# Half-precision filter weights and spectrum matrices, both orders' last filter weights prepared together, and the conditioning matmuls inside the first filter spectrum

## The chip, the core and the metric

The kernel runs on one core of a Trainium2 chip. The metric is the device time of one execution in microseconds (us). It is written with an explicit instruction stream per engine: TensorE (PE) for matmuls, with weight loads of its own (PEld), VectorE (DVE), ScalarE (ACT), GpSimd (POOL), and SyncE (SP), which here only issues DMAs. Each engine takes its instructions strictly in order, and an instruction that waits for a semaphore holds up everything behind it on the same engine.

## What is computed

A two-layer diffusion backbone over 1024 latent tokens and 256 context tokens of 1024 channels. The part that the change touches is the head of layer 0: the long filters of the Hyena half, their spectra, the conditioning vectors and the first norm.

```python
def hyena_filters(L, w1, b1, freq, w2, b2, w3):
    ...
    h = jnp.sin(freq * (z @ w1 + b1))
    h = jnp.sin(freq * (h @ w2 + b2))
    h = (h @ w3).reshape(L, 2, HY_ORDER, HY_CH)
    ...
    h = h * jnp.exp(-t01 * deltas)[:, None, None, :]
    h = h / jnp.sum(jnp.abs(h), axis=(0, 1), keepdims=True)
    ...

def long_conv(u, filt, skip):
    L = u.shape[1]
    uf = jnp.fft.rfft(u, n=2 * L, axis=1)
    ff = jnp.fft.rfft(filt, n=2 * L, axis=0)
    y = jnp.fft.irfft(uf * ff[None], n=2 * L, axis=1)[:, :L]
    return y + u * skip

def reference(x, c, ctx, c_ctx, ada_w, ada_b, norm1_g, ...):
    ...
        sh1, sc1, g1, sh2, sc2, g2 = ada_mod(c, ada_w[i], ada_b[i])
        u_lat = modulate(rms_norm(h_lat, norm1_g[i]), sh1, sc1)
    ...
            y_lat = mixer_ab(u_lat, *ab)
```

`ada_mod` is silu(c) times a 1024 x 6144 matrix. `mixer_ab` starts with an input projection of the normed and modulated tokens; two long convolutions follow (orders 0 and 1), each with a filter that does not depend on the tokens. There is one filter for the latent length ("l", 1024) and one for the context length ("c", 256), with the same weights.

## The kernel before

The filters' spectra are matmuls with stored cosine and sine matrices. To keep nearly fp32 accuracy a value is split in two parts, hi and lo (ACT copies the rounded hi, DVE subtracts it: the helper `split`, lines 287 and 289), and products are made for hi and lo apart. In this kernel the filter part works in fp32r, a rounded fp32 type of four bytes; the input projection works with pairs of f16 values.

The first 200 us of the kernel run as follows.

1. `filter_mlp`: two layers of matmul and Sin (line 592) over 640 positions, latent and context together. The result is split into `ta` and `tb` (lines 599 to 602).
2. `ada_first`: the first 2048 columns of the conditioning matrix for both conditions, 16 tiles of 512 KB from `in_ada_k`, loaded on POOL's queue into a pool of two large buffers (`mat`) and multiplied two rows at a time (line 423, 64 matmuls with 2 stationary columns). Four of its eight steps stand ahead of the raw filter, the rest are dealt into it. Then the four result rows are copied by ACT (`g`, line 431), turned into columns by 32 small matmuls, and joined with bias and gain (lines 438, 441); `operand_scale` takes the greatest entries over all partitions with an all-reduce on POOL (line 1238) and makes the scale columns that every norm needs.
3. `filter_raw` of order 0: loads the last filter weights `w3`, makes sum and difference (line 626), splits them, and for each of 4 blocks and 2 halves multiplies with `ta` or `tb` and with the window `in_win_l` (DVE, line 646).
4. `filter_spectrum` of order 0, with `filter_raw` of order 1 dealt into it, one step a yield: 16 operands (4 kinds i by 4 blocks b), each a sum or difference of two raw pieces (line 713 and its neighbours), split in hi and lo, against a 128 x 1024 matrix `in_ff_l`. That matrix comes from memory as f16 and is cast to fp32r by ACT first (line 335, into `mat`). Each order also needs a sum of absolute values over the filter, `filter_sum`: Abs on ACT (lines 658, 659), a maximum and a running sum on DVE (lines 660, 662; three sums an order), and small matmuls with a column of ones that bring it to one number per channel; DVE then inverts it (lines 678 to 681). From its twelfth step on the first norm is dealt in (`norms`: squares of the rows of x on ACT, line 2149; scaled tokens on DVE and ACT, lines 555 to 558).
5. `filter_spectrum` of order 1 with the rest of the norm.
6. `in_proj`, the input projection (f16, line 283 with `wh` and `wl`), with the context filters and more conditioning dealt into it. The context filters load `w3` again and make sum and difference on POOL (line 626) and the splits again.

All matmuls go through the helper `mm` (line 283), all SP loads through `ld` and all POOL loads through `ldr` (line 274). Names in the trace are pools: `s` holds tiles of 128x512 and 128x1024, `t` and `tk` short-lived tiles, `mat`, `wh`, `wl` large weight buffers, `c` small columns, `ps` and `pq` PSUM.

Of the kernel before, what the change touches and what calls it, by code (L numbers as in the profile page):

```python
# [19 lines left out]
P = 128  # L20
# [12 lines left out]
PAD_C, PAD_T, SHIFT = 176, 160, 16  # L33
# [168 lines left out]
class Builder:  # L202
# [117 lines left out]

    def cmat(self, w, src, view=None, small=False, shift=False):
# [86 lines left out]
    def ada_first(self):  # L408
# [7 lines left out]
        for kb in range(KB):  # L416
            ws = [self.mat(1024, F32) for _ in range(2)]
# [148 lines left out]
    def filter_mlp(self):  # L566
# [12 lines left out]
        for layer, w in enumerate((w1, w2)):  # L579
            s = self.S4(F32, 640)  # L580
            for c0, cw in ((0, 512), (512, 128)):
                ps = self.PS()
                self.mm(ps[:, :cw], w, x[:, c0:c0 + cw], True, True)
                nc.vector.tensor_scalar(s[:, c0:c0 + cw], ps[:, :cw], vec[:, layer:layer + 1], vec[:, 2:3],
                                        op0=ADD, op1=MUL)
            n = self.S4(F32, 640)
# [6 lines left out]
            x = s  # L593
        self.tap("mlp", x)
        self.ta, self.tb = {}, {}
        for sq, c0, cw in (("l", 0, 512), ("c", 512, 128)):
            ta, tb = self.S2(F32R, cw), self.S2(F32R, cw)
            cs = slice(c0, c0 + cw)
            nc.scalar.copy(ta[0:64], x[0:64, cs])
            nc.vector.tensor_tensor(ta[64:128], x[0:64, cs], ta[0:64].bitcast(F32), SUB)  # L600
            nc.scalar.copy(tb[64:128], x[64:128, cs])
            nc.vector.tensor_tensor(tb[0:64], x[64:128, cs], tb[64:128].bitcast(F32), SUB)
# [3 lines left out]
        self.alt = self.C(4, F32R)  # L606
# [3 lines left out]
        self.frg, self.rn, self.kap = {}, {}, {}  # L610

    def filter_raw(self, sq, raws, os=(0, 1)):
# [3 lines left out]
        w3, st = {}, {}  # L616
        for o in os:
            for j in (0, 1):
                st[(o, j)] = self.S2()
                self.ld(st[(o, j)], a["w3"][:, (2 * j + o) * HC:(2 * j + o + 1) * HC])  # L620
        if sq == "l":
            yield
        for o in os:
            for eo, op in ((0, ADD), (1, SUB)):
                t = self.T()
                (nc.vector if sq == "l" else nc.gpsimd).tensor_tensor(t, st[(o, 0)], st[(o, 1)], op)
                hi, lo = self.S2(F32R), self.S2(F32R)
                self.split(t, hi, lo)
                w3[(o, eo)] = (hi, lo)
        for b in range(nb):  # L630
            for s, lh in ((0, self.ta[sq]), (1, self.tb[sq])):
                w = self.S2()
                self.ld(w, a["win_" + sq][b, s])
# [16 lines left out]
    def filter_sum(self, sq, o, raw):  # L650
# [3 lines left out]
        if sq == "l":  # L654
            acc = self.S4()
            for b in range(nb):
# [4 lines left out]
                if b:  # L661
                    nc.vector.tensor_tensor(acc, acc, t, ADD)
# [21 lines left out]
    def filter_spectrum(self, sq, o, raw):  # L684
# [8 lines left out]
        fh = (self.S2(F32R), self.S2(F32R))  # L693
        nc.scalar.copy(fh[0][0:1, :], re[0:1, :])
        nc.vector.tensor_tensor(fh[1][0:1, :], re[0:1, :], fh[0][0:1, :].bitcast(F32), SUB)
# [5 lines left out]
        def operands():  # L701
            for i in range(4):
                for b in range(nb):
# [8 lines left out]
                    else:  # L712
                        (nc.vector if sq == "l" else nc.gpsimd).tensor_tensor(t, f, r, ADD if i in (0, 3) else SUB)
# [1408 lines left out]
    def run(self):  # L2122
# [17 lines left out]
        def norms():  # L2140
# [6 lines left out]
            with self.follow(self.last_hi):  # L2147
                for i, t in rows:
                    nc.scalar.activation(t, t, AF.Square, accum_out=sq[:, i:i + 1])
# [42 lines left out]
        mlp, fr = self.filter_mlp(), self.filter_raw("l", raws["l"], (0,))  # L2192
# [3 lines left out]
        next(fr)  # L2196
        next(ng)
        drain(mlp)
        for _ in range(4):
            next(ada1)  # L2200
        with self.tc.issue_after(self.clamp), self.tc.issue_after(self.sin):
            next(fr)
        for i, _ in enumerate(fr):
            next(ada1, None)
            if i in (0, 4):
                next(ng)
        drain(ada1)
        self.u0col, self.usi = self.operand_scale(0, 0, (0, 1))
# [303 lines left out]
```

## Time and profile before

| what | us |
|---|---|
| median of the runs shown (2914.33, 2919.48, 2921.39) | 2919.48 |
| the profiled execution | 2919.95 |
| its span | 2918.2 |
| PE busy over the span | 2766.6 (95%) |
| DVE busy | 2094.0 (72%) |
| ACT busy | 1647.7 (56%) |
| POOL busy | 642.6 (22%) |
| first spectrum's first matmul | 69.44 |
| second spectrum's first matmul | 140.74 |
| input projection's first matmul | 205.69 |

Times in the trace count from the span's start. Rows of a timeline give start, duration, engine, line of the kernel, operation, output and inputs by pool names, shapes and count, and in brackets how long the engine stood idle just before and what released it. Rows of stretches give the busy time of each engine with its number of instructions, then the clock that TensorE was granted as a share of full speed, the busy share of the DMA engines and GB/s. Matmul ends are modelled, so a row of one matmul shows its latency; the pace is read from the starts of successive rows.

### The profile page before, as it was taken

The page shows a single profiled execution, that of the slowest core. Times are in us where ns is not written, and L with a number is a line of the kernel's source. Part 1 is how long each engine was busy: PE and PEld are TensorE (multiplying, and loading weights), DVE is VectorE, ACT ScalarE, POOL GpSimd, SP SyncE. Part 2 cuts the span into 40 slices and gives each one's busy share as a digit, 9 for nine tenths or more (in the row PEclk, how much of TensorE's full clock was granted, in tenths as well). Part 3 has the DMA queues.
Part 4 walks back from the last instruction along what each step waited for, and adds up shares of the span by engine and source line. Part 5 has one row for each costly group of instructions (what it writes and reads, how often), then busy time and mean ns, then how long its engine had stood idle before and what let it go on. Part 6 is the DMA issues. An engine that isn't in the chain of part 4 may idle for free. (4 is left out here: it accounts for less than half of the span.)

```text
span 2918.2 us, 46050 instructions
## 1 busy us (share of the span) xinstructions
PE 2766.6 (95%) x16163; PEld 1714.2 (59%) x16163; DVE 2094.0 (72%) x3833; ACT 1647.7 (56%) x2899; POOL 642.6 (22%) x1057
## 2 busy tenths in 40 slices
PE   6989999999989999999999999999999999999998
PEld 3766557888879644444555844676665444444554
DVE  4778867585467798877886767776676778775765
ACT  4674324454675667654555555676664477654553
POOL 1012013354220121213120012444443022112000
PEclk8989999999999999999999999999999999999999
DMA  6574434358785555566994798777775666424753
GB/s 254 187 265 161 161 122 151 111 168 286 285 344 182 207 205 197 201 213 240 327 333 161 273 337 294 179 188 172 185 198 188 236 226 231 153 93 184 242 191 113
DMA packets 325156, 615.98 MB, mean 211 GB/s; under 512 B 90934, under 2 KB 130552, under 8 KB 324922
## 3 DMA queue, kind: packets, MB, share of 16 engines
q1 hardware_dynamic: 252378, 384.38, 39.9%
q0 software_dynamic: 70240, 224.45, 21.6%
q10 hardware_dynamic: 2304, 4.20, 0.4%
q8 instruction: 127, 2.08, 0.3%
q14 instruction: 107, 0.88, 0.1%
HBM read 455.33 MB, written 135.53 MB: 202 GB/s over the span
## 5 line engine op out<-in xcount | busy, mean ns | idle before, releaser
L1449 PE MATMUL ps<-s,s 128*128 128x512 f16 x2592 | 582.2, 382 | 14.4 <-ACT tk L1454 6.8
L1449 PEld LDWEIGHTS <-s 128*128 128x128 f16 x2640 | 259.0, 98 | 332.6 <-issue 27.8
L283 PE MATMUL ps<-s,wh 128*128 128x256 f32 (+3 forms) x1752 | 398.2, 331 | 11.1 <-ACT wh L287 5.4
L1218 ACT ACTIVATE s<-s,c 128x512 f16<-128x512 f32 (+1 forms) x324 | 233.5, 754 | 141.9 <-DMA s<-d 79.9
L1219 DVE SCALAR_TENSOR_TENSOR s<-s,c,s 128x512 f16<-128x512 f32 (+1 forms) x324 | 247.4, 794 | 84.5 <-ACT s L1218 84.1
L1666 PE MATMUL ps<-s 128*128 128x512 f16 (+2 forms) x1308 | 303.4, 378 | 2.0 <-DVE s L1219 2.0
L283 PE MATMUL pq<-s,wh 128*128 128x512 f16 (+1 forms) x1000 | 280.3, 354 | 9.8 <-DMA wh<-d 5.4
L283 PE MATMUL ps<-s,wl 128*128 128x256 f32 (+3 forms) x876 | 261.6, 331 | 1.3 <-DVE wl L289 1.2
L283 PEld LDWEIGHTS <-wh 128*128 128x128 f16 x1664 | 160.9, 99 | 170.2 <-issue 20.9
L1666 PEld LDWEIGHTS <-s 128*128 128x128 f16 x1536 | 148.5, 98 | 178.9 <-issue 6.5
L274 POOL DMA_DIRECT2D d<-s x201 | 109.0, 543 | 640.5 <-DVE s L1510 178.6
L283 PE MATMUL ps<-s,s 128*128 128x65 f16 (+5 forms) x2666 | 222.3, 236 | 27.5 <-DMA s<-s 11.4
L335 ACT CAST mat<-cs 128x1024 fp32r<-128x1024 f16 (+2 forms) x120 | 111.6, 935 | 140.6 <-PE ps L283 57.3
L283 PEld LDWEIGHTS ps<-s,wh 128*128 128x128 f32 x1088 | 177.5, 192 | 18.1 <-ACT wh L287 5.7
L283 PE MATMUL ps<-s,mat 128*128 128x512 f32 x696 | 184.7, 413 | 3.3 <-DVE s L289 2.9
L1449 PE MATMUL ps<-s,wh 128*128 128x512 f16 x616 | 184.9, 379 | 1.8 <-DVE g L1463 1.4
L283 PE MATMUL pq<-s,wl 128*128 128x512 f16 (+1 forms) x500 | 174.5, 354 | 0.5 <-DMA wl<-d 0.5
L283 PEld LDWEIGHTS <-s 128*128 128x128 f16 x2400 | 114.5, 98 | 82.9 <-DMA s<-s 11.5
L283 PEld LDWEIGHTS ps<-s,mat 128*128 128x128 f32 x696 | 136.5, 199 | 37.9 <-DVE s L289 3.8
L1251 ACT ACTIVATE t<-s 128x1024 bf16<-128x1024 f32 (+1 forms) x164 | 141.9, 867 | 12.2 <-DVE c L470 8.4
L283 PEld LDWEIGHTS ps<-s,s 128*128 128x128 f32 (+1 forms) x746 | 113.6, 192 | 32.1 <-ACT s L287 7.0
L283 PEld LDWEIGHTS <-wl 128*128 128x128 f16 x832 | 82.3, 99 | 77.4 <-issue 4.5
(431 smaller groups left out, 5477.3 us busy)
## 6 DMA issues: line engine op xcount, KB each, us to landing
s<-d SPq DMA_DIRECT2D x294, 256.0 KB, 4.0
d<-s POOLq DMA_DIRECT2D x157, 256.0 KB, 3.2
s<-in_down SPq DMA_DIRECT2D x154, 256.0 KB, 5.4
s<-in_ada_w POOLq DMA_DIRECT2D x48, 512.0 KB, 4.8
g<-in_bias POOLq DMA_DIRECT2D x128, 192.0 KB, 3.6
s<-in_gate SPq DMA_DIRECT2D x46, 512.0 KB, 3.7
s<-in_up SPq DMA_DIRECT2D x46, 512.0 KB, 4.0
d<-g POOLq DMA_DIRECT2D x87, 256.0 KB, 2.9
```

What stands on the lines that cost most here:

```text
L274: self.last_ldr = self.nc.gpsimd.dma_start(out, in_).ins
L283: self.nc.tensor.matmul(o, l, r, start=st, stop=sp)
L335: self.nc.scalar.copy(m, st)
L1218: nc.scalar.activation(hi, src, AF.Copy, scale=scale)
L1219: nc.vector.scalar_tensor_tensor(lo, src, scale, hi, op0=MUL, op1=SUB)
L1251: self.nc.scalar.activation(junk[:, :t.shape[1]], t, AF.Abs, scale=2.0 ** -15, accum_out=st[:, k:k + 1])
L1449: nc.tensor.matmul(ps, x[:, sl], y, start=first and j == 0 and x is wh and y is xh, stop=j == 3 and x is wl, skip_group_check=True)
L1666: m = nc.tensor.matmul(acc[j][:, c0:c1], x[:, sl], y[:, xs], start=first and k == 0, stop=last and k == 2, skip_group_check=True)
```

## The change

Types: `ta`, `tb`, the alternating signs and the splits of the filter part become f16 (`split16`: hi and lo halves of one f16 tile), and `in_ff_l` is loaded as f16 straight into the matmul's buffer (`mat16`, three buffers) without a cast. The casts of line 335 fall away for the filters' matrices: 32 for the latent ones, and small ones for the context.

Weights: a new `filter_w3` loads `w3` of both orders and the first two windows, finds a scale from the column sums of absolute values (Abs on ACT, matmuls with ones, a maximum on DVE), makes the four sums and differences on DVE, splits them into f16 pairs, and writes these to device memory (`w3d`) through POOL's queue. `filter_raw` takes them from there; the context filters read `w3d` back and prepare nothing.

Order: `ada_first` is dealt into the first eight steps of the first spectrum, with buffers from the large `s` pool in place of `mat`; its end and `operand_scale` follow at the ninth. The squares of the norm go one by one where the program puts them. The running sum of `filter_sum` moves from DVE to POOL, and so do the sums of order 1 in blocks 0 and 2 that have no mask (5 of 16).

```diff
-PAD_C, PAD_T, SHIFT = 176, 160, 16
+PAD_C, PAD_T, SHIFT = 168, 160, 16
...
+    def mat16(self, w):
+        self.m16 = (getattr(self, "m16", 0) + 1) % 3
+        return self.pw.tile([P, w], F16, tag=("ws", "wh", "wl")[self.m16], name=self.nm("m16"))
...
-            ws = [self.mat(1024, F32) for _ in range(2)]
+            ws = [self.S4() for _ in range(2)]
...
-        self.sgn = self.S2(F32R)
+        self.sgn = self.S2(F16)
...
+        self.w3d = {(o, eo): self.DR([P, 1024], F16) for o in (0, 1) for eo in (0, 1)}
+
+    def split16(self, src):
+
+        t = self.S2(F16, 1024)
+        self.nc.scalar.copy(t[:, :512], src)
+        self.nc.vector.tensor_tensor(t[:, 512:], src, t[:, :512], SUB)
+        return t[:, :512], t[:, 512:]
+
+    def filter_w3(self):
...
+        for o in (0, 1):
+            ab = self.T(BF16, 1024)
+            ps = sums[o] = self.PS()
+            for j in (0, 1):
+                nc.scalar.activation(ab[:, j * 512:j * 512 + 512], st[(o, j)], AF.Abs)
+            for j in (0, 1):
+                self.mm(ps, self.ones.bitcast(BF16)[:, 1::2], ab[:, j * 512:j * 512 + 512], j == 0, j == 1)
+        yield
...
+        for o in (0, 1):
             for eo, op in ((0, ADD), (1, SUB)):
                 t = self.T()
+                nc.vector.tensor_tensor(t, st[(o, 0)], st[(o, 1)], op)
+                x = self.S2(F16, 1024)
+                self.half_split(t, big[:, o:o + 1], x[:, :512], x[:, 512:])
+                self.ldr(self.w3d[(o, eo)], x)
+                self.w3[(o, eo)] = (x[:, :512], x[:, 512:])
+            yield
...
                 if b:
-                    nc.vector.tensor_tensor(acc, acc, t, ADD)
+                    nc.gpsimd.tensor_tensor(acc, acc, t, ADD)
...
-                        (nc.vector if sq == "l" else nc.gpsimd).tensor_tensor(t, f, r, ADD if i in (0, 3) else SUB)
-                    xh, xl = self.S2(F32R), self.S2(F32R)
-                    self.split(t, xh, xl)
-                    yield xh, xl, self.cmat(2 * nb * P, a["ff_" + sq][i, b])
+                        eng = nc.vector if sq == "l" and (o == 0 or b % 2) else nc.gpsimd
+                        eng.tensor_tensor(t, f, r, ADD if i in (0, 3) else SUB)
+                    xh, xl = self.split16(t)
+                    mt = self.mat16(2 * nb * P)
+                    self.ld(mt, a["ff_" + sq][i, b])
+                    yield xh, xl, mt
...
         fr = self.filter_raw("l", raws["l"], (1,))
         for i, _ in enumerate(self.filter_spectrum("l", 0, raws["l"][0])):
+            if i < 8:
+                next(ada1)
+            elif i == 8:
+                drain(ada1)
+                self.u0col, self.usi = self.operand_scale(0, 0, (0, 1))
             if i >= 2:
                 next(fr, None)
-            if i >= 11:
+            if i < 4 or i >= 11:
                 next(ng)
```

On ACT, at the head of the program, before (`s_44` and `s_48` are the states of the two filter layers, the rows of line 2149 the squares of the norm):

```order
L592 ACTIVATE s_44_142<-s_44_142 128x640
L592 ACTIVATE s_48_157<-s_48_157 128x640
L599 CAST s_52_172<-s_48_157 64x512
L601 CAST s_53_173<-s_48_157 64x512
L599 CAST s_54_178<-s_48_157 64x128
L601 CAST s_55_179<-s_48_157 64x128
L287 CAST s_71_225<-t_223 128x512
L287 CAST s_74_231<-t_229 128x512
L2149 ACTIVATE s_34_122,c_265<-s_34_122 128x1024
```

The second Sin stands right behind the first, and the squares come after the splits. Now, in the same place (Sin is line 598, the squares line 2200, the hi copy of `ta` line 607):

```order
L2200 ACTIVATE s_42_138,c_241<-s_42_138 128x1024
L598 ACTIVATE s_48_150<-s_48_150 128x640
L2200 ACTIVATE s_43_140,c_241<-s_43_140 128x1024
L2200 ACTIVATE s_44_142,c_241<-s_44_142 128x1024
L2200 ACTIVATE s_45_144,c_241<-s_45_144 128x1024
L2200 ACTIVATE s_46_146,c_241<-s_46_146 128x1024
L2200 ACTIVATE s_47_148,c_241<-s_47_148 128x1024
L2202 ACT_TABLE_LOAD
L2202 ACTIVATE c_241<-c_241,c_95 128x10
L598 ACT_TABLE_LOAD
L598 ACTIVATE s_58_182<-s_58_182 128x640
L607 CAST s_62_197<-s_58_182 64x512
```

The first Sin stands among the squares, and the second behind all ten of them, a square root and two table loads.

On POOL, behind the conditioning loads, before (line 1238 is the all-reduce, its first row sets the engine up for it):

```order
L274 DMA mat_329<-in_ada_k 128x1024
L1238 ISA
L1238 ISA c_425<-c_425 128x1
L274 DMA s_553_1698<-in_cg_l 128x256 x2
L626 ISA
L626 TENSOR_TENSOR t_1831<-s_588_1823,s_589_1825 128x512
L626 TENSOR_TENSOR t_1837<-s_588_1823,s_589_1825 128x512
L626 TENSOR_TENSOR t_1843<-s_590_1827,s_591_1829 128x512
L626 TENSOR_TENSOR t_1849<-s_590_1827,s_591_1829 128x512
```

The all-reduce is the only computation on POOL until line 626, in the input projection. Now (line 711 is the running sum of order 0 in `s_238`, line 1290 the all-reduce, line 764 sums of order 1):

```order
L274 DMA s_227_706<-in_ada_k 128x1024
L711 TENSOR_TENSOR s_238_734<-s_238_734,s_256_815 128x1024
L1290 ISA
L1290 ISA c_783<-c_783 128x1
L711 ISA
L711 TENSOR_TENSOR s_238_734<-s_238_734,s_264_850 128x1024
L711 TENSOR_TENSOR s_238_734<-s_238_734,s_269_875 128x1024
L764 TENSOR_TENSOR t_1086<-s_208_663 128x512
L764 TENSOR_TENSOR t_1223<-s_208_663 128x512
L764 TENSOR_TENSOR t_1274<-s_150_456 128x512
L764 TENSOR_TENSOR t_1350<-s_210_668 128x512
```

The all-reduce stands between the first and the second sum of order 0, and the engine is set up for it and set back in between.

On PE, toward the end of the first spectrum, before (`ps_973` is the column sum of the running sum `s_254_779`, `s_300` and `s_301` hi and lo of an operand):

```order
L283 MATMUL ps_932<-s_300_936,mat_942 128x512
L283 MATMUL ps_933<-s_300_936,mat_942 128x512
L283 MATMUL ps_973<-c_91,s_254_779 128x1 x8
L283 MATMUL pq_930<-s_301_937,mat_942 128x512
L283 MATMUL pq_930<-s_300_936,mat_942 128x512
L283 MATMUL ps_931<-s_301_937,mat_942 128x512
L283 MATMUL ps_931<-s_300_936,mat_942 128x512
L283 MATMUL ps_932<-s_301_937,mat_942 128x512
L283 MATMUL ps_932<-s_300_936,mat_942 128x512
```

The running sum comes from DVE, and 32 matmuls of the first spectrum stand behind the column sum. Now (`ps_948` is the column sum, `s_289_943` hi and lo of the operand):

```order
L283 LDWEIGHTS m_290_946
L283 MATMUL ps_913<-s_289_943,m_290_946 128x512
L283 LDWEIGHTS m_290_946
L283 MATMUL ps_914<-s_289_943,m_290_946 128x512
L283 MATMUL ps_948<-c_91,s_238_734 128x1 x8
L283 LDWEIGHTS m_290_946
L283 MATMUL ps_911<-s_289_943,m_290_946 128x512
L283 LDWEIGHTS m_290_946
L283 MATMUL ps_911<-s_289_943,m_290_946 128x512
L283 LDWEIGHTS m_290_946
L283 MATMUL ps_912<-s_289_943,m_290_946 128x512
```

The column sum, which now waits for the last of POOL's three sums, stands ahead of the last 20 matmuls of the first spectrum.

More of the change, by code (lines that the diff above doesn't have):

```diff
@@ L585, in filter_mlp @@
                                         op0=ADD, op1=MUL)
+            if layer == 0:
+                yield
             n = self.S4(F32, 640)
@@ L593, in filter_mlp @@
             x = s
+            if layer == 0:
+                yield
         self.tap("mlp", x)
@@ L2146, in norms @@
             sq = self.C(10)
-            with self.follow(self.last_hi):
-                for i, t in rows:
-                    nc.scalar.activation(t, t, AF.Square, accum_out=sq[:, i:i + 1])
+            for i, t in rows:
+                nc.scalar.activation(t, t, AF.Square, accum_out=sq[:, i:i + 1])
+                yield
             nc.scalar.activation(sq, sq, AF.Sqrt, scale=1.0 / D, bias=self.eps)
```

84 lines of the change are left out of this document (51 added, 33 removed).

## The prediction

> **What bounds the kernel now.** The change works at the head, so I read the table of stretches first, cut at the first matmul of each stage.
>
> ```profile
> core 0: us, PE busy (x) PEld busy (x) DVE busy (x) ACT busy (x) POOL busy (x), PEclk, DMA share, GB/s
> 0.00:42.50 42.50, 19.63 (x70) 8.66 (x70) 22.26 (x40) 20.18 (x40) 9.21 (x23) 0.90 0.95 360
> 42.50:69.40 26.90, 21.20 (x73) 10.88 (x72) 6.02 (x25) 9.68 (x17) 1.97 (x4) 0.65 0.37 118
> 69.40:140.70 71.30, 64.00 (x258) 50.13 (x258) 51.16 (x86) 43.88 (x64) 0.00 (x0) 0.90 0.51 169
> 140.70:198.20 57.50, 54.53 (x226) 42.22 (x227) 49.39 (x77) 46.99 (x70) 1.28 (x2) 0.94 0.65 223
> 198.20:211.60 13.40, 6.07 (x18) 2.56 (x18) 4.74 (x10) 10.13 (x18) 2.94 (x2) 0.62 1.01 382
> 211.60:460.00 248.40, 241.02 (x1340) 138.08 (x1339) 194.78 (x406) 86.55 (x155) 41.12 (x50) 0.98 0.42 152
> ```
>
> Up to 42.5 us the DMA engines are full (0.95). From 42.5 to 69.4 no engine but PE is busy, with 73 matmuls in 27 us at a granted clock of 0.65. Then two spectra of 71.3 and 57.5 us, in which DVE has 51 and 49 us of work beside PE. From 211.6 on PE is the bound (241 of 248 us), and what the head gains passes on almost unchanged. The timeline of ACT and PE tells what the second stretch is.
>
> ```profile
> 24.05 0.74 ACT L592 ACTIVATE s<-s 128x640 f32<-128x640 f32 x1 [7.56 <-DVE s L591]
> 27.42 0.79 PE L283 MATMUL ps<-s,s 128*128 128x512 f32 x1 [5.86 <-ACT s L287]
> 32.38 1.90 PE L423 MATMUL ps<-mat,c 128*2 128x512 f32 x16
> 52.37 3.08 PE L423 MATMUL ps<-mat,c 128*2 128x512 f32 x8 [2.91 <-DMA mat<-in_ada_k]
> 56.21 6.96 PE L283 MATMUL ps<-c,g 2*128 2x2 f32 x32 [0.77 <-ACT g L431]
> 63.10 1.22 PE L283 MATMUL ps<-t,c 128*128 128x256 f32 x2
> 64.11 3.62 PE L283 MATMUL ps<-tk,c 128*128 128x512 f32 x4
> 69.44 0.39 PE L283 MATMUL ps<-s,c 128*2 128x512 f32 x1 [0.51 <-ACT s L287]
> ```
>
> The raw products start 3.4 us after the second Sin; then PE waits for the conditioning tiles one after the other, up to 55.4, turns the rows into columns, and only then starts the first spectrum. So 42.5 to 69.4 is a chain of latencies, not work.
>
> **The change, part by part.**
>
> *The front.* The second Sin now stands behind ten squares of the norm, a root and two table loads. A square is 1.05 us and a load 1.28 us here:
>
> ```profile
> 27.79 1.06 ACT L2149 ACTIVATE s<-s 128x1024 f32<-128x1024 f32 x1
> L413 ACT ACT_TABLE_LOAD x1 | 1.3, 1283 | 0.7 <-PEq L2499 0.7
> GB/s 0 32 217 349 373 392 359 247 415 418 423 418 421 423 412 420 407 411 411 418 410 388 402 395 406 396 421 330 104 16 74 295 341 343 232 105 8 5 0 31
> s<-in_x_row SPq DMA_DIRECT2D x10, 512.0 KB, 9.8
> 5.57 10.73 SPq L268 DMA_DIRECT2D s<-in_x_row  x10
> ```
>
> The tenth row of x is what matters. Ahead of it on SP's queue stand now 1.0 MB more of w3 and windows, but the conditioning tiles no longer share the DMA engines: they wait on POOL's queue behind the w3d writes. About 7.5 MB (ten rows of 0.52 MB, six tiles of 0.26 MB, the rest small) have to land; the slices of 1.5 us of the first 60 us in the DMA view add up to this at about 22.8 us; square, loads and root (1.05 + 0.2 + 1.28 + 0.3 + 1.28) put the Sin at 27.0, 3 us later than now. From there the raw products start 3.4 us later as now, two more pairs are split on DVE (1.4), 16 window products follow (0.62 apart: 9.9), then the first row's pieces and the operand sums that stand ahead in DVE's queue (some 7 us of ten instructions like L713), and hi, lo and their waits (3.3): 52.0 us for the first spectrum's start instead of 69.44. The preparation of w3 (four Abs, matmuls with ones, sums and splits) lies ahead of the second Sin, where ACT waited 7.56 us and PE 5.86; it costs nothing while w3 lands before the rows of x, and each us of delay beyond that costs one. If the tenth row lands as late as now plus the added bytes (issued at 16.3 us, 9.8 us to landing, then 1.0 MB at 415 GB/s, 2.5: 28.6), the Sin comes at 32.7 and the start at 58.
>
> *To the first running sum.* Now DVE makes the first of these at 116.40, 46.96 after the spectrum's start. What comes in: 64 conditioning matmuls at 0.12 us (1.90 for 16: 7.6); the columns and the row sums, which took 6.96 and 1.22 + 3.62 at clock 0.65 and take 0.65/0.95 of it at full clock (8.1); some 2 us of waits in their chain PE, ACT, PE, DVE. What goes out: f16 in place of fp32r.
>
> ```profile
> 100.98 2.96 PE L283 MATMUL ps<-s,mat 128*128 128x512 f32 x12
> 103.78 1.56 PE L283 MATMUL pq<-s,mat 128*128 128x512 f32 x6
> 213.01 0.59 PE L283 MATMUL ps<-s,wl 128*128 128x512 f16 x2
> 213.55 0.59 PE L283 MATMUL ps<-s,wh 128*128 128x512 f16 x2
> L335 ACT CAST mat<-cs 128x1024 fp32r<-128x1024 f16 x32 | 33.4, 1051 | 34.0 <-issue 12.4 <-PE ps L283 10.4 <-PE ps L423 5.2
> ```
>
> Twelve fp32r matmuls take 2.80 us (0.233 each); three f16 ones of 1280 columns together 0.54 (0.216 per 512). So 185 matmuls save 3.1 us; the type alone is worth little, since f16 and fp32r run at nearly one pace. The 32 casts (33.4 us) leave ACT, which was never the last to be waited for by much; that is worth something only where ACT holds DVE up. First running sum: 52 + 46.96 + 7.6 + 8.1 + 2 - 3.1 = 113.6 us.
>
> *The sums and the all-reduce on POOL.* This is what the change adds. Its prices:
>
> ```profile
> 476.64 2.55 POOL L901 TENSOR_TENSOR t<-t,t 128x512 f32<-128x512 f32 x2 [22.36 <-DVE t L900]
> 413.33 1.79 POOL L848 TENSOR_TENSOR s<-s,s 128x512 f32<-128x512 f32 x1
> 420.85 0.38 POOL L1238 PARTITION_ALL_REDUCE c<-c  x1 [5.73 <-issue]
> 421.26 0.15 DVE L1239 TENSOR_SCALAR c<-c 128x1 f32<-128x1 f32 x1 [6.13 <-POOL c L1238]
> 431.07 1.27 POOL L852 TENSOR_TENSOR s<-s 128x128 f32<-128x128 f32 x1 [9.85 <-issue]
> L662 DVE TENSOR_TENSOR s<-s,s 128x1024 f32<-128x1024 f32 x6 | 7.3, 1211 | 0.0
> ```
>
> A 512-wide sum is 1.27 us on POOL, so a 1024-wide one is about 2.55 (DVE: 1.21). Where an all-reduce follows a tensor operation, POOL stands 5.73 us with nothing to wait for, and DVE waits 6.13 for it. In the head of the kernel before, this set-up is hidden, since POOL does nothing else there. Now the first sum stands ahead of it and two more behind it. DVE does only some 4 us of work meanwhile and then stops at the reduce's result, with eight pieces of the norm and the lo halves of the last two operands behind it, for which PE waits. From the first sum (0): sum to 2.55, set-up to 8.28, reduce to 8.66; DVE goes on, norms start at about 9.2 (at 122.8; now 122.14). Setting POOL back for the sums is priced nowhere: between 0.1 us (nothing) and 5.7 us (as much as the other way; the 9.85 us ahead of 431.07 hold other waits too and don't tell). I take half, 2.9. The second and third sum end at 8.66 + 2.9 + 5.1 = 16.7. PE's column sum waits for this, at the head of PE's queue, with 20 matmuls (4.3 us) behind it; with 1.0 us for the column sum the second spectrum starts at 113.6 + 22.0 = 135.6 us, with the bounds 132.8 and 138.4. That is 5.1 us before the 140.74 of now: of 17.4 us gained in front, 12.3 are given back.
>
> [...]
>
> *The second spectrum.*
>
> ```profile
> 140.74 0.39 PE L283 MATMUL ps<-s,c 128*2 128x512 f32 x1 [2.70 <-ACT s L287]
> L713 DVE TENSOR_TENSOR t<-s 128x512 f32<-128x512 f32 x24 | 16.0, 680 | 0.0
> L626 POOL TENSOR_TENSOR t<-s,s x4: 1266/1760/2246, 208.7 to 213.3; 128x512 f32<-128x512 f32 x4
> 211.15 1.09 DVE L289 TENSOR_TENSOR s<-t,s 128x512 fp32r<-128x512 f32 x1 [1.80 <-ACT s L287]
> 212.17 2.29 DVE L470 CUSTOM_DVE_ANT_0 s<-s,s 128x1024 f32<-128x1024 f32 x1
> 214.39 2.28 DVE L470 CUSTOM_DVE_ANT_0 t<-s,s 128x1024 bf16<-128x1024 f32 x1
> 218.41 1.21 DVE L470 CUSTOM_DVE_ANT_0 s<-s,s 128x1024 f32<-128x1024 f32 x1
> ```
>
> DVE works 49.4 of 57.5 us now and is the bound together with its waits for ACT. It loses three sums (1.21) and five operand sums (0.68): 7.0. But POOL's operations slow it: while POOL made four 512-wide sums, three DVE instructions took 1.09, 2.29 and 2.28 us instead of 0.68, 1.21 and 1.21, that is 2.6 us, or 0.64 a sum. Five of these and three of double width cost 7.0: a draw. The 8.1 us in which DVE was not busy should shrink, since 16 casts of 1.05 us leave ACT's 47 us and hi copies come sooner; I take 4.6. So 49.4 + 4.6 = 54 us, and the end is 135.6 + 54 = 189.6 instead of 198.2: 8.6 us.
>
> *The input projection.* Four POOL sums with their slowing of DVE (2.6) and four lo parts on DVE (2.7) go. PE's waits for DVE there are these:
>
> ```profile
> PE ps L283 <- DVE c L1316: 3.8, 1, 3.8
> PE ps L867 <- DVE s L289: 3.4, 1, 3.4
> ```
>
> Between nothing and 3.8 us of that goes; I take 2.5, as the work is spread over more than these two places. The rest of the kernel keeps its order but for small shifts: nothing, within 2 us.
>
> **Sum.** 8.6 + 2.5 = 11.1 us against the profiled execution of 2919.95 us (0.5 us over the median of the runs shown): 2908.9, so 2909 us. Its own range, from the bounds of setting back, of the projection and of the shifts: 2903 to 2916.
>
> **Rivals.**
>
> *ACT was what held DVE up.* For it: both waits of PE before the spectra end at ACT's hi copies (2.70 us at 140.74), and 33 us leave ACT. Then the second spectrum runs at DVE's bare 49.4 us, setting back is free (132.8), and it ends at 182.2: 16.0 gained, and 3.8 in the projection: 2900. Against it: the norms' chain DVE, ACT, DVE stays.
>
> *The tenth row of x comes late.* The Sin at 32.7 as above, the spectrum's start at 58: 6 us less gain, 2915. For it: DMA is full in that time; against it: the conditioning tiles, 8.4 MB, start later than now.
>
> *POOL costs more than it saves: slower.* The place is POOL from its first sum to the end of the second spectrum. Setting back takes 5.7 us (start at 138.4), and each POOL sum blocks DVE for its whole length, 5 x 1.27 + 3 x 2.55 = 14.0 instead of 7.0, while DVE's idle 8.1 us stay, as the norms wait for ACT and DMA as before: 42.4 + 14.0 + 8.1 = 64.5. The end is at 202.9, 4.7 us later than now; the projection gives nothing: 2925. It decides from a second spectrum of 60 us on. For it: POOL itself took up to 2.25 us for 1.27. Against it: DVE's 2.29 for 1.21 are less than a whole sum.
>
> [...]
>
> **How the numbers follow.** Below 0.3% (8.8 us) a measurement of this kernel can't be told from no change; the forecast lies just beyond it. Chances: forecast 0.45, ACT relief 0.17, late row 0.13, POOL dearer 0.20, and 0.05 for shifts elsewhere. Faster by over 0.3% (below 2911): 0.27 of the forecast's 0.45, 0.17 of the relief, 0.02 more: 0.46. Slower by over 0.3% (above 2929): 0.10 of POOL dearer (late row and POOL together give 2931) and 0.03 more: 0.13. The rest is 0.41. The range takes in the relief and the POOL case: 2898 to 2927.
>
> **What would show it.** Right: the first spectrum starts at 50 to 55 us; DVE stands about 4 to 5 us before the reduce's result; PE stands before the column sum for several us; the second spectrum starts at 133 to 138 and lasts about 54 us. Wrong: a second Sin after 31 us (late row); a second spectrum under 51 us (relief) or over 60 (POOL); a gap between the reduce and the second sum of under 1 us or over 6; or the input projection growing.

## The result and the profile after

The change makes the kernel slightly slower. Over 20 runs each, the median is 2923.16 us (2915.45 to 2932.81) against 2913.79 us before (2905.21 to 2925.07); the ratio is 1.0028 with a 95% interval of 1.0018 to 1.0038, about 8 us. The profiled execution took 2932.81 us (span 2931.0), the highest of the 20, so stages are compared here at places in the head, not by the span.

The stretches of the profile after, cut at the first matmul of each stage and at PE's waits between the spectra (columns as in the stretches of before):

```profile
0.00:50.90 50.90, 17.34 (x44) 6.29 (x45) 31.80 (x58) 26.82 (x48) 9.76 (x24) 0.97 0.88 322
50.90:120.00 69.10, 68.30 (x298) 25.46 (x297) 30.06 (x52) 26.56 (x44) 3.15 (x6) 0.92 0.57 193
120.00:131.70 11.70, 4.99 (x25) 2.33 (x25) 6.89 (x17) 1.13 (x3) 2.72 (x2) 0.93 0.21 67
131.70:141.60 9.90, 1.86 (x4) 0.40 (x3) 5.25 (x12) 1.72 (x4) 5.50 (x3) 0.50 0.00 0
141.60:154.00 12.40, 10.56 (x36) 6.02 (x37) 3.33 (x10) 3.08 (x7) 1.18 (x1) 0.64 0.21 71
154.00:213.90 59.90, 53.95 (x226) 22.16 (x226) 52.23 (x71) 35.67 (x57) 23.37 (x9) 0.89 0.64 213
213.90:221.80 7.90, 0.35 (x3) 0.04 (x2) 0.66 (x5) 7.90 (x16) 0.00 (x0) 0.80 1.03 417
221.80:470.00 248.20, 243.92 (x1354) 137.93 (x1355) 193.90 (x407) 83.81 (x147) 36.20 (x47) 0.97 0.46 159
```

The first spectrum starts at 50.9 us instead of 69.4. But from 120.0 to 141.6 PE runs 29 matmuls in 21.6 us, and from there to 154.0 only 36 more; the granted clock is 0.50 from 131.7 on and 0.64 in the last of these stretches. From 131.7 to 141.6 no engine is busy for more than 5.5 of the 9.9 us: it is a chain of waits, the same picture that 42.5 to 69.4 gave before, in another place. The timeline of POOL names it:

```profile
120.08 2.34 POOL L711 TENSOR_TENSOR s<-s,s 128x1024 f32<-128x1024 f32 x1 [38.19 <-issue]
128.75 0.38 POOL L1290 PARTITION_ALL_REDUCE c<-c  x1 [6.33 <-issue]
136.02 5.55 POOL L711 TENSOR_TENSOR s<-s,s 128x1024 f32<-128x1024 f32 x2 [6.89 <-issue]
```

The first running sum, 6.33 us in which POOL waits for nothing on record, the all-reduce, 6.89 us of the same, and two more sums up to 141.57. What hangs on it, on DVE and on PE:

```profile
120.78 1.73 DVE L1286 SCALAR_TENSOR_TENSOR c<-c 128x1 f32<-128x1 f32 x2
129.16 0.15 DVE L1291 TENSOR_SCALAR c<-c 128x1 f32<-128x1 f32 x1 [4.31 <-POOL c L1290]
145.23 0.16 DVE L727 COPY c<-ps 128x4 f32<-128x4 f32 x1 [8.28 <-PE ps L283]
```

```profile
50.93 0.58 PE L283 MATMUL pq<-s,c 128*2 128x512 f16 x1 [6.56 <-ACT s L624]
120.28 4.71 PE L283 MATMUL ps<-s,m 128*128 128x512 f16 x21
131.74 1.86 PE L283 MATMUL ps<-s,m 128*128 128x512 f16 x4 [6.76 <-ACT s L624]
141.62 3.57 PE L283 MATMUL ps<-c,s 128*128 128x1 f32 x16 [8.01 <-POOL s L711]
145.05 7.12 PE L283 MATMUL ps<-s,m 128*128 128x512 f16 x20
154.01 0.38 PE L283 MATMUL pq<-s,c 128*2 128x512 f16 x1 [1.84 <-ACT s L624]
221.76 2.31 PE L283 MATMUL ps<-s,wh 128*128 128x256 f16 x6 [1.72 <-ACT wh L1270]
```

DVE stops for the reduce, and with it the operands of the spectrum: PE stands 6.76 us. Then PE stands 8.01 us for the last sum on POOL, and DVE 8.28 us for PE. The 20 matmuls that the program has behind the column sum stand with it: the last hi and lo halves made for them (lines 624 and 625) were done at 132.2 and 135.2 us, and they start at 145.05. When PE goes on, its granted clock is 0.50 (141.6 to 145.05): the column sum takes 3.57 us, and 20 f16 matmuls take 7.12 us, where 20 at the pace of before take 4.3. (e1 below shows that the second of these two prices doesn't hang on the long stops.) So the 18.5 us gained in front turn into 13.3 us lost at the second spectrum's start (154.01 against 140.74) and 16.1 at the projection's start (221.76 against 205.69). The projection up to the first matmul of line 919 (line 867 before) takes 248.2 us instead of 254.0, which leaves 10.3 us. That is the measured loss within its uncertainty.

### The profile page after: what moved, and what is told of

Same layout as the page of the kernel before. It is cut to its first block, busy times and chain, and to the rows that moved or that the text cites. A ratio compares the mean times of both kernels' runs of the same rounds, so it can differ in the third digit from the quotient of the medians.

```text
span 2931.0 us, 45984 instructions
## 1 busy us (share of the span) xinstructions
PE 2765.4 (94%) x16167; PEld 1664.1 (57%) x16167; DVE 2087.2 (71%) x3822; ACT 1614.8 (55%) x2860; POOL 665.1 (23%) x1068
## 3 DMA queue, kind: packets, MB, share of 16 engines
q0 software_dynamic: 70560, 225.37, 21.7%
## 5 line engine op out<-in xcount | busy, mean ns | idle before, releaser
L1501 PEld LDWEIGHTS <-s 128*128 128x128 f16 x2640 | 258.7, 98 | 328.4 <-issue 22.5
L283 PE MATMUL ps<-s,wh 128*128 128x256 f32 (+3 forms) x1848 | 406.0, 328 | 10.8 <-ACT wh L287 7.8
L283 PE MATMUL ps<-s,wl 128*128 128x256 f32 (+3 forms) x924 | 268.5, 328 | 1.2 <-DVE wl L289 1.2
L283 PE MATMUL pq<-s,wh 128*128 128x512 f16 (+1 forms) x904 | 254.4, 362 | 5.5 <-DVE s L2007 2.4
L1718 PEld LDWEIGHTS <-s 128*128 128x128 f16 x1536 | 148.4, 98 | 179.0 <-issue 6.5
L283 PEld LDWEIGHTS <-s 128*128 128x128 f16 (+1 forms) x2500 | 124.6, 98 | 109.4 <-issue 23.6
L283 PE MATMUL pq<-s,wl 128*128 128x512 f16 (+1 forms) x452 | 159.8, 362 | 0.0
L1270 ACT ACTIVATE s<-t,c 128x512 f16<-128x512 f32 x174 | 116.3, 711 | 21.1 <-DVE c L1369 9.8
L339 ACT CAST mat<-cs 128x1024 fp32r<-128x1024 f16 (+2 forms) x80 | 74.7, 941 | 94.8 <-PE ps L283 27.5
L1271 DVE SCALAR_TENSOR_TENSOR s<-t,c,s 128x512 f16<-128x512 f32 x174 | 124.9, 747 | 1.6 <-ACT s L1270 1.6
L1501 PE MATMUL ps<-s,wl 128*128 128x512 f16 x308 | 116.5, 379 | 0.0
```

The lines of the kernel that those rows point to most:

```text
L283: self.nc.tensor.matmul(o, l, r, start=st, stop=sp)
L339: self.nc.scalar.copy(m, st)
L1270: nc.scalar.activation(hi, src, AF.Copy, scale=scale)
L1271: nc.vector.scalar_tensor_tensor(lo, src, scale, hi, op0=MUL, op1=SUB)
L1501: nc.tensor.matmul(ps, x[:, sl], y, start=first and j == 0 and x is wh and y is xh, stop=j == 3 and x is wl, skip_group_check=True)
L1718: m = nc.tensor.matmul(acc[j][:, c0:c1], x[:, sl], y[:, xs], start=first and k == 0, stop=last and k == 2, skip_group_check=True)
```

## The experiments

Eleven runs of ten kernels were made, each beside the kernel before on the same chip. The table gives the starts of the two last stages of the head and of the first matmul of line 919 or its counterpart, from one profile each, and the ratio of the times to before. "Reduce early" and the other names are explained below.

| kernel | second spectrum | projection | line 919 | ratio to before (95%) |
|---|---|---|---|---|
| before | 140.74 | 205.69 | 459.7 | |
| the change | 154.01 | 221.76 | 470.0 | 1.0028 (1.0018 to 1.0038) |
| e1, all running sums on DVE | 142.34 | 207.49 | 456.1 | 0.9971 (0.9957 to 0.9986) |
| e2, order 0's sums on DVE | 141.10 | 209.15 | 457.2 | 1.0018 (1.0004 to 1.0032) |
| e9, the same again | 141.76 | 209.89 | 459.9 | 1.0027 (1.0012 to 1.0042) |
| e12, two of order 0's sums on DVE | 148.69 | 216.55 | 463.8 | 1.0039 (1.0025 to 1.0054) |
| e4, operand sums on DVE | 151.89 | 223.99 | 473.1 | 1.0067 (1.0050 to 1.0084) |
| e5, reduce early | 134.15 | 202.60 | 452.1 | 0.9968 (0.9955 to 0.9982) |
| e6, reduce early, sums on DVE | 134.35 | 199.32 | 448.5 | 0.9954 (0.9938 to 0.9971) |
| e11, reduce early, all on DVE | 134.38 | 199.44 | 449.7 | 0.9959 (0.9944 to 0.9975) |
| e8, conditioning in front | 141.55 | 209.70 | 458.4 | 0.9997 (0.9987 to 1.0008) |
| e7, before with sums on POOL | 134.33 | 203.90 | 457.2 | 1.0031 (1.0016 to 1.0045) |
| e10, before with f16 spectra | 133.67 | 197.01 | 448.0 | 0.9995 (0.9978 to 1.0012) |

The theory: POOL's set-up for the all-reduce and back, with the running sums around it, is on the path of DVE and PE and costs what the front gained. Its main rival: POOL's sums and DVE hold each other up, spread over both spectra.

### All running sums on DVE (e1)

```diff
-                    nc.gpsimd.tensor_tensor(acc, acc, t, ADD)
+                    nc.vector.tensor_tensor(acc, acc, t, ADD)
```

> All six running sums back on DVE, all else as in the change. Theory (POOL's set-up, reduce, set-back and two sums, 21.5 us from the first sum to the column sum, hold DVE and PE): the column sum comes at about 127 us instead of 141.6, PE does not cool down, the second spectrum starts at about 136 instead of 154.0, and the time falls by 14 to 18 us against the change, to about 6 to 8 us below the kernel before. [...] Rival (what is gained in front is lost in the projection whatever happens in between): under 4 us.

The ratio goes from 1.0028 to 0.9971, 16.6 us: the theory's 14 to 18. In the profiles 11.7 us of it stand at the second spectrum's start and 13.9 at line 919. The column sum comes at 127.64 (PE's timeline):

```profile
127.64 1.91 PE L283 MATMUL ps<-c,s 128*128 128x1 f32 x16
133.35 7.16 PE L283 MATMUL ps<-s,m 128*128 128x512 f16 x20 [1.92 <-DVE s L625]
142.34 0.38 PE L283 MATMUL pq<-s,c 128*2 128x512 f16 x1 [1.84 <-ACT s L624]
```

The second spectrum starts 6 us later than expected: the 20 matmuls behind the column sum still take 7.16 us, as in the change (7.12), so that the expected "PE does not cool down" was wrong: the granted clock falls here, too. The stretches of this run show that the long stops aren't needed for it:

```profile
112.00:120.00 8.00, 7.23 (x36) 4.90 (x35) 3.96 (x11) 7.75 (x11) 0.00 (x0) 0.68 0.56 191
133.30:140.60 7.30, 7.16 (x20) 2.54 (x20) 6.04 (x13) 1.36 (x3) 1.57 (x1) 0.62 0.12 36
```

The clock is low from the conditioning's 32 small column matmuls on (0.68), and again after two stops of only 0.86 and 1.92 us (0.62). Behind the column sum it falls in before and in e11, too, where PE stood only 2.61 and 1.03 us ahead of it: 0.50 from 129 to 132 us in before, 0.79 from 120 to 128 in e11. What the long stops of the change add to this is the column sum at a granted clock of 0.50, 3.57 us instead of 1.91.

### Order 0's sums on DVE, twice (e2, e9)

```diff
-                    nc.gpsimd.tensor_tensor(acc, acc, t, ADD)
+                    (nc.gpsimd if o else nc.vector).tensor_tensor(acc, acc, t, ADD)
```

> Only order 0's three running sums back on DVE; order 1's stay on POOL. Theory: nearly all of the loss stands between the first and the second spectrum, so 12 to 16 us below the change and within 5 us of the run with all six on DVE; the second spectrum keeps its 60 us. [...]

> Order 0's sums on DVE once more, beside the others on one chip. In its profile the input projection started only 1.7 us later than with all six on DVE, while its median was 12.7 us higher. Theory (the rest is spread of TensorE's granted clock after the head): now within 6 us of all six on DVE, about 0.1 to 0.2% below the kernel before. If order 1's sums on POOL cost something real further down: again 0.1 to 0.3% above it.

A miss, twice, and on two chips. In the head the theory holds: the second spectrum starts at 141.10 and 141.76, the projection some 2 us after e1's. But the medians stay at 1.0018 and 1.0027: of e1's 16.6 us below the change no more than 3, and the second is the number of e9's rival (again 0.1 to 0.3% above before). What makes the difference comes for the greater part after the projection's start. The granted clock lies between 0.975 and 0.984 from run to run, and within the runs of e2 and of e9 a difference of 0.002 goes with 2 and 4 us. This stays open, below.

### Two of order 0's three sums on DVE (e12)

```diff
-                    nc.gpsimd.tensor_tensor(acc, acc, t, ADD)
+                    (nc.vector if o == 0 and b < 3 else nc.gpsimd).tensor_tensor(acc, acc, t, ADD)
```

> Order 0's first two running sums on DVE, the third on POOL, where it stands ahead of the all-reduce; order 1's stay on POOL. So the set-up for the reduce stays on DVE's path and the set-back goes off the column sum's path. Theory: DVE stands 6 to 8 us before the reduce's result (2.5 us sum, 5.7 to 6.3 us set-up), the column sum comes at about 129 us, the second spectrum starts at 146 to 149, between the change (154.0) and order 0's sums all on DVE (141.1 and 141.8). If only the set-back and the late column sum hurt: the second spectrum starts within 2 us of 141.5.

This takes the set-up for the reduce apart from the set-back. Rows of the timelines of POOL, DVE and PE:

```profile
125.73 2.34 POOL L711 TENSOR_TENSOR s<-s,s 128x1024 f32<-128x1024 f32 x1 [43.48 <-PE ps L283]
134.20 0.38 POOL L1290 PARTITION_ALL_REDUCE c<-c  x1 [6.13 <-issue]
134.61 0.15 DVE L1291 TENSOR_SCALAR c<-c 128x1 f32<-128x1 f32 x1 [8.95 <-POOL c L1290]
137.20 1.86 PE L283 MATMUL ps<-s,m 128*128 128x512 f16 x4 [7.13 <-ACT s L624]
148.69 0.38 PE L283 MATMUL pq<-s,c 128*2 128x512 f16 x1 [1.84 <-ACT s L624]
```

One sum ahead of the reduce, and DVE stands 8.95 us (6 to 8 were expected), PE 7.13 behind it. The second spectrum starts at 148.69, inside the expected 146 to 149: the set-up with one sum is worth 7.3 us against e2 and e9 (141.4), the set-back with the other two sums 5.3 us more. The total time doesn't follow: 1.0039 is no lower than the change's 1.0028, although line 919 comes 6.1 us earlier.

### The reduce early (e5), and with the sums on DVE too (e6)

```diff
-            if i < 8:
+            if i < 4:
                 next(ada1)
-            elif i == 8:
+                next(ada1)
+            elif i == 4:
                 drain(ada1)
```

> The conditioning steps go two to a step of the first spectrum, and the all-reduce comes at its fifth step, ahead of all running sums, which stay on POOL. Theory: set-up and set-back (6.3 and 6.9 us) are hidden, the three sums remain; the second spectrum starts at about 141 (13 us earlier), and the time falls by 10 to 13 us against the change. If POOL's slow sums and not the set-ups are the cost: 3 to 5 us only. If the conditioning tiles arrive too late for this order: PE waits for them in the first 30 us of the spectrum.

> The early all-reduce and all six running sums on DVE together. Theory: with the reduce early, set-up and set-back are hidden already, so taking the sums off POOL adds only what the column sum still waits (0.5 us) and the 3 us that order 1's sums on POOL cost the second spectrum: 2 to 5 us below the early reduce alone. If the set-ups are not the cost but the sums: as much gain as the sums on DVE brought to the change, 13 to 17 us.

With POOL still making all sums, but the reduce ahead of them, the ratio is 0.9968, 17.5 us below the change; the expected 10 to 13 was too low. POOL's and PE's rows of e5:

```profile
96.04 0.38 POOL L1290 PARTITION_ALL_REDUCE c<-c  x1 [37.37 <-DVE c L1289]
112.45 9.24 POOL L711 TENSOR_TENSOR s<-s,s 128x1024 f32<-128x1024 f32 x3 [16.03 <-PE ps L283]
134.15 0.38 PE L283 MATMUL pq<-s,c 128*2 128x512 f16 x1 [1.84 <-ACT s L624]
```

The reduce starts as soon as its input is there, at 96.0, and 16 us pass before the first sum is wanted: both set-ups are hidden. The second spectrum starts 19.9 us earlier than in the change, and not all of that is POOL's. From the first running sum to the second spectrum e5 takes 21.7 us and the change 33.9: 12.2 less, near the expected 13. Another 6.6 come ahead of the first running sum, which stands 62.5 us behind the first spectrum's start instead of 69.15, and 1.0 from the front. The earlier conditioning is part of the edit: its 64 matmuls stand in larger groups and keep PE busy for 10.9 us instead of 13.8.

With the sums on DVE as well (e6) it is 0.9954, some 4 us less, as expected: 3.3 us of it show at the projection's start, though the two intervals overlap. This is the lowest ratio of the study, 13 us below before.

The four kernels together take the two parts of the edit apart. With the reduce late, POOL's sums cost 11.7 us at the second spectrum's start (154.01 in the change, 142.34 in e1); with the reduce early, nothing (134.15 in e5, 134.35 in e6). And where POOL makes no running sum at all, the early conditioning with its reduce still brings that start from 142.34 to 134.35, 1.1 of it from the first spectrum's start.

### Operand sums on DVE (e4, e11)

```diff
-                        eng = nc.vector if sq == "l" and (o == 0 or b % 2) else nc.gpsimd
+                        eng = nc.vector if sq == "l" else nc.gpsimd
```

e4 is the change with this edit, e11 is e6 with it.

> Only the operand sums of order 1 back on DVE; the running sums stay on POOL. Theory: the set-up, the reduce and the order 0 sums stand as they are, the second spectrum starts at 154 as in the change; 0 to 3 us faster than the change. [...]

> Early all-reduce, running sums and operand sums all on DVE: POOL has nothing but the reduce until the projection. Theory: the run with only the operand sums on DVE lost 4.4 us in its second spectrum against the change, so five operand sums on POOL are a gain; 2 to 5 us slower than the early reduce with the running sums on DVE. [...]

The main rival falls in this place: without POOL's five operand sums the second spectrum up to the projection takes 72.1 us in e4 against 67.75 in the change, longer and not shorter. The theory missed, too: 0 to 3 us faster were expected, and e4's median, 1.0067, loses 11 us against the change, of which 3.1 show at line 919. In e11 the price is 1 us or so, a little under what was expected, and the second spectrum up to the projection is no longer than in e6 (65.06 and 64.97).

### Before with the sums on POOL (e7)

```diff
-                    nc.vector.tensor_tensor(acc, acc, t, ADD)
+                    nc.gpsimd.tensor_tensor(acc, acc, t, ADD)
```

> The kernel before with one part of the change alone: the six running sums on POOL. The all-reduce stands ahead of them by 50 us there. Theory: set-up and set-back stay hidden, DVE gains 3.6 us an order and loses about as much by sharing: within 4 us of before. Rival (sums on POOL cost by themselves): 8 us or more slower than before.

```profile
59.07 0.38 POOL L1238 PARTITION_ALL_REDUCE c<-c  x1 [12.05 <-DVE c L1237]
112.15 5.77 POOL L662 TENSOR_TENSOR s<-s,s 128x1024 f32<-128x1024 f32 x2 [1.23 <-DVE s L660]
117.97 2.08 PE L283 MATMUL ps<-c,s 128*128 128x1 f32 x16 [1.31 <-POOL s L662]
```

In the profile the set-ups are hidden and the column sum waits 1.31 us, no more. In that execution the conditioning came early and the first spectrum started at 63.90 instead of 69.44; from there to the projection it took 140.0 us against 136.25, 3.8 more, inside the expected 4. (The loss by "sharing" in this expectation is an estimate from the prediction's rows around 212 us of before, 0.64 us of DVE for each 512-wide sum on POOL, so 3.8 for an order's three of double width.) The median is 9 us above before, though, which is the rival's number. The profiled execution was the fastest of 12 (2913.19 us, median 2926.38), so the profile can't settle it.

### The conditioning in front again (e8)

```diff
         for i, _ in enumerate(self.filter_raw("l", raws["l"], (0,))):
+            next(ada1, None)
...
+        drain(ada1)
+        self.u0col, self.usi = self.operand_scale(0, 0, (0, 1))
```

The same steps are left out of the first spectrum.

> The change with the conditioning dealt into the raw filter of order 0 again, ahead of the first spectrum, and the all-reduce with it; sums stay on POOL. The first spectrum starts at 66 to 72 us, since the conditioning tiles are loaded behind the w3 writes. If the place of the conditioning is worth what its matmuls and columns cost inside the spectrum (15 and 6 us, against the 17 to 20 us of waiting in front): within 5 us of the early reduce. If the front gain is real and kept: 10 us or more slower than the early reduce.

The last conditioning tile is used at 62.23 and the first spectrum starts at 69.25, 19.3 us after e5's. Yet the second starts only 7.4 us after e5's, and the ratio is 0.9997 against 0.9968, 8.5 us. Neither expectation hits; the truth lies between: of the gain in front more than half is spent again on the conditioning's matmuls and columns inside the spectrum, and some 7 us are kept. Part of these 7 is another wait: PE stands 4.71 us for POOL's last sum before e8's column sum, and 0.53 in e5.

### Before with f16 in the spectra alone (e10)

```diff
-                    xh, xl = self.S2(F32R), self.S2(F32R)
-                    self.split(t, xh, xl)
-                    yield xh, xl, self.cmat(2 * nb * P, a["ff_" + sq][i, b])
+                    xh, xl = self.split16(t)
+                    mt = self.mat16(2 * nb * P)
+                    self.ld(mt, a["ff_" + sq][i, b])
+                    yield xh, xl, mt
```

with f16 signs, and with w3 and the raw products left in fp32r.

> The kernel before with the spectra's types alone: operands and matrices in f16, no casts of the matrices; conditioning, sums, w3 and order stay as before, and w3 and the raw products stay fp32r. Theory (as in the prediction): the pace of a matmul is nearly the same, 480 of them save at most 8 us of PE time, and ACT is freed of 33 us that were hidden: 3 to 8 us faster, most of it in the second spectrum. Rival (ACT held DVE up): the second spectrum runs at DVE's 49 us, and 10 us or more are gained. Rival (types are worth nothing): within 2 us.

```profile
66.39 0.38 PE L283 MATMUL ps<-s,c 128*2 128x512 f16 x1 [0.78 <-ACT s L328]
133.67 0.38 PE L283 MATMUL ps<-s,c 128*2 128x512 f16 x1 [1.84 <-ACT s L328]
197.01 0.39 PE L283 MATMUL pq<-s,wh 128*128 128x256 f16 x1 [2.76 <-ACT wh L1231]
```

The first spectrum takes 67.3 us instead of 71.3, the second with the way to the projection 63.3 instead of 64.95: 5.6 us, as the theory had it, though most of it in the first spectrum and not in the second. A third buffer for the matrices came with the types. The comparison of the times, 0.9978 to 1.0012, can't tell this from nothing: the medians differ by the rival's under 2 us, the head of the profile by the theory's 5.6.

## Why the prediction was wrong

Forecast were 2909 us, 11 us faster; measured is about 8 us slower, the other direction. By its own steps:

**The front: right, in part by luck.** Forecast was the first spectrum's start at 52 us, measured 50.93. The second Sin came at 30.24 instead of 27.0, between the forecast and the late case of 32.7, but the work behind it took 20.7 us instead of 25.0, so that two errors nearly cancel.

**To the first running sum: mis-sized.** Forecast 113.6, measured 120.08. From the first spectrum's start that is 69.15 us where 61.6 were added up. The conditioning's 64 matmuls were taken at 0.12 us, from a row in which two tiles run together (1.90 us for 16). In the spectrum they mostly stand four by four:

```profile
74.13 1.04 PE L427 MATMUL ps<-s,c 128*2 128x512 f32 x8
75.10 1.98 PE L283 MATMUL ps<-t,c 128*128 128x512 f32 x4
77.67 1.03 PE L427 MATMUL ps<-s,c 128*2 128x512 f32 x4
78.62 1.47 PE L283 MATMUL ps<-s,m 128*128 128x512 f16 x6
```

By the starts of successive rows four of one tile hold PE for 0.95 us, 0.24 each, as long as eight of two tiles (0.97). The first 20 stand together and take 3.45. With nine groups of four that makes 13.0 us where 7.6 were counted: 5.4 of the 7.6 that are missing. Another 1.6 come from seven f16 matmuls right behind the first small column matmuls (115.85 to 118.94 us), which take 3.1 us at a granted clock of 0.50 instead of 1.5 at the pace of before.

**Set-up and reduce: right.** 5.73 was forecast; 6.33, 6.13 (e12) and 5.62 (e4) were measured. e12 shows that it holds DVE (8.95 us) and through it PE (7.13).

**The step that failed: from the first running sum to the second spectrum.** The prediction added up 22.0 us (113.6 to 135.6); measured are 33.9 (120.08 to 154.01). This is just enough to turn the forecast gain of 11 us into a loss. Two of its terms are at fault, the set-back and what follows the column sum.

**The set-back: mis-sized.** It was bounded by 0.1 and 5.7 us and taken as 2.9. Measured are 6.89 in the change and 7.62 in e4, past the upper bound, which had no reason behind it but that the other way takes as much. With it the sums end 21.5 us after the first one starts instead of 16.7. A gap of over 6 us at this place was one of the prediction's own signs of being wrong.

**What follows the column sum: mostly missing.** Forecast were 1.0 us for the column sum and 4.3 for 20 matmuls; the second spectrum started 12.4 us after the wait. PE had stood for 6.76 and 8.01 us, and its clock was 0.50 and 0.64 of full speed; the column sum took 3.57 us (1.91 in e1), the matmuls 7.12, and 1.84 us of wait for ACT followed. The prediction had read a low clock in the stretch 42.5 to 69.4 of before (0.65) and didn't carry it to this place. A forecast without the two long stops would have missed most of this, too: in e1, with stops of 0.86 and 1.92 us, the 20 matmuls take 7.16 us, in e5 and e6 6.16 and 5.91, and the 1.84 us for ACT stand in all of them. Only the slow column sum, some 1.7 us, goes with the long stops here. What lowers the clock wasn't tried; small matmuls stand ahead of it in each of these runs, the 32 columns or the column sum.

The three shortfalls together move the second spectrum's start from the forecast 135.6 to 154.0: 6.5 before the first sum, 4.8 on POOL, 7.1 behind it.

**The second spectrum: too short.** Forecast 54 us to its end, measured 59.9, with DVE busy for 52.2 of them. POOL's sums of order 1, with two instructions of DVE beside them, show how the two engines hold each other up:

```profile
174.66 2.83 DVE L764 TENSOR_TENSOR tk<-s 128x512 f32<-128x512 f32 x1
185.47 1.21 DVE L709 TENSOR_TENSOR s<-s,s 128x1024 f32<-128x1024 f32 x1
```

```profile
174.21 2.74 POOL L711 TENSOR_TENSOR s<-s,s 128x1024 f32<-128x1024 f32 x1 [1.22 <-issue]
179.44 13.21 POOL L711 TENSOR_TENSOR s<-s,s 128x1024 f32<-128x1024 f32 x2 [2.49 <-DVE s L709]
```

An operand sum on DVE that takes 0.68 us elsewhere took 2.83 beside POOL's sum of 174.21 to 176.95. Then it was POOL that stood back: 13.21 us for two sums that take 4.7 alone, of which the first has 10.78 (179.44 to 190.22) and the second 2.35. DVE worked without a pause up to 188.0, and the first sum ended 2.2 us after that, about the length of one sum. In e4 the same sum took 2.67 us. But taking order 1's sums to DVE shortens this stage by only 2 to 3 us (e1 65.15 us to the projection, e2 and e9 68.05 and 68.13, the change 67.75), and taking the operand sums there lengthens it by 4.4 (e4). So the rival in which each sum on POOL blocks DVE for its whole length was wrong in size: no run shows its 14.0 us for all eight; the runs show these 2 to 3 us, and a loss where the operand sums go. The draw that was forecast was about right. What is also left of the 5.9 us is a granted clock of 0.89 instead of 0.94 in this stretch; what lowers it wasn't tried.

**The projection: right in kind, mis-sized.** Forecast 2.5 us, bounds 0 and 3.8; measured 5.8 (248.2 against 254.0), and between 247.3 and 250.2 in all kernels made from the change.

**The rivals.** The slower case, POOL dearer than what it saves with set-back in full, had the place right and 20% of the chance. Its price, 2925 us, was near the measured 2923, but by another sum: it had the second spectrum start at 138.4 and put the loss into DVE. That the number came near is luck.

**Open.** Measured against before, e2, e9, e12, e4, e7 and e10 have medians 6 to 12 us higher than their place at line 919 would give; e1 lies 5 us lower, the others within some 2 us. All of the six but e10 have order 1's sums on POOL, but so have e5, e8 and the change, which fit, and e10 has none of these sums on POOL. The profiles of e7 and e12 are those of their fastest executions, so that their places say little about their medians. Those of e2 and e9 show that much of it arises far behind the head: e2 stands 1.1 us behind e1 at line 919, 4.5 at the last matmul of line 2114 (2218.5 us in e1) and 9.6 at the end of the span, e9 3.8, 7.7 and 11.1, with the same 16167 matmuls in all three; POOL's sums of the two orders end at about 182 us. The granted clock differs from run to run (0.975 to 0.984 within e9). No run here shows the cause. So the places in the head show that order 0's sums around the reduce cost the front's gain, and the times of e1, e5, e6 and e11 agree; the times of e2, e9 and e12 don't.

## What to carry to other kernels

An operation that is free where it stands can become the bound when another kind of work is put beside it on the same engine: the all-reduce held DVE up for 0.55 us in before (line 1239 at 64.58), where POOL had nothing else to do, and brought 13 us of set-up and set-back in the change (6.33 and 6.89), where a sum stood on each side of it. So count switches, not instructions, when work goes to POOL, and put the odd operation ahead of the rest, as e5 does. Its 17 us less include what the earlier conditioning brings by itself, 8 us at the second spectrum's start where POOL makes no running sum (e1 against e6). And don't forecast the matmuls behind a wait at full pace: 20 that take 4.3 us at the pace of before took between 5.9 and 7.2 in the change, e1, e5 and e6, after stops of 1.35 to 8 us, and 4.5 in e11, after one of 0.65.

## What was not expected of the hardware

Setting POOL back from the all-reduce to sums took longer (6.89 and 7.62 us) than setting it up (5.62 to 6.33). Two tiny DVE instructions with two inputs (L1286, 128x1) took 1.73 us together while POOL's sum ran (0.22 in e1, where it didn't), and ended as the sum ended (122.5 and 122.4 us); a sum on POOL beside a run of DVE without a pause took 10.78 us, and 2.34 at 120.08. Matmuls with two stationary columns took 0.12 us each where eight of two tiles (0.97 us, the change) or 16 of several (1.90 us, before) stood together, and 0.24 where one tile's four stood alone (0.95 us, the change). The granted clock fell to 0.50 behind small matmuls (the change, 115.85 to 118.94 us), with no idle time of PE on record since 111.7.
